# The first twenty projections of layer 0 in two halves of the contraction, with partial sums in DRAM and the second half's modulation on VectorE

## The chip, the cores and the metric

The kernel runs on one core of a Trainium2 chip. The metric is the time of one execution on the device in microseconds (us); the median of three runs is given. One execution was also recorded by the hardware profiler: its span runs from the first to the last instruction.

## What is computed

A trunk of two layers over 768 tokens (512 latent, 256 context) of width 2048. Cut to what matters here, each layer does this:

```python
shift, scale, gate = split(silu(c) @ ada_w + ada_b, 3)      # one vector for latent, one (c_ctx) for context tokens
h  = rms_norm(x, norm_w) * (1 + scale) + shift
p  = h @ w_in                                               # 2048 -> 8192 columns, split into twelve parts
y  = concat(gmlp(p), hgrn2_both_directions(p), diff_attention(p))
x  = x + gate * (y @ w_out)
```

The last layer's context output isn't needed, so many of its projections are 512 tokens wide, the rest and all of layer 0's are 768 wide. All of it is fp32: each matmul operand is split into a high and a low part, and a product is three matmuls (high x high, high weight x low, low weight x high).

## The kernel before

Activations lie transposed: a tile holds 128 features of all tokens. The contraction of 2048 is 16 tiles ("kt"), and the normalised, modulated input of a layer is 16 pairs hi0/lo0 to hi15/lo15. One projection makes 128 output columns for all tokens in an accumulator "pp" of 128x768 in PSUM (two of them): `mm_group` (line 383) issues, for each kt of a group of four, the three products, each as a matmul of 512 tokens and one of 256 with the same weights. That is 48 pairs for a projection. Weights come in quarters (four kt): a DMA into "raw", a ScalarE cast to "wh" (line 318), and a VectorE subtraction to "wl" (line 319), five buffers each.

Jobs of layer 0, in program order: four Hgrn units of five projections (two gates, query, output gate, value: projections 0 to 19), four Attn units of eight, the Gmlp unit, then 16 output projections. A unit's own work hangs on its projections. For Hgrn this is a scan in seven levels (lines 566 to 610): small TensorE products (line 581), masked copies and a product on VectorE (590, 599), three products on GpSimd (601, 603, 604) and a ScalarE copy back (569); then transposes and state products.

The modulation needs `silu(c) @ ada_w`, 24 blocks of 256 columns for each layer, 2 MB each. Layer 0's shift and scale (blocks 0 to 15) must be there before its h tiles. They run on TensorE (`ada_pe`, matmuls in line 250, then a VectorE copy in line 260 and lines 210 and 215 that finish the vector): two ahead of everything, then one for each kt while the first four projections run in the "lead", kt by kt, each four groups behind one new h tile (`h_tile`: VectorE 308, ScalarE 311, VectorE 312, for 512 and 256 tokens). The other 32 blocks (layer 0's gates and all of layer 1) run on VectorE (`ada_dve`, line 266): per block eight loads "adas" of 256 KB in two buffers, four accumulations (lines 275, 277) for each, a transpose (283) and a reduction (285). They are stepped as filler behind each job of layer 0, FILL steps of one kt each: 8 behind an Hgrn job, 7 Attn, 4 Gmlp, 9 behind an output projection.

A scheduler with a timing model sets the order of instructions on each engine; DMAs are issued by SyncE, in program order up to `pinned[0] = False`.

Of the kernel before, what the change touches and what calls it, by code (L numbers as in the profile page):

```python
# [33 lines left out]
MASKS = 5  # L34
FWD = (4, 5, 0, 1, 2, 3)
# [12 lines left out]
def trunk(  # L48
# [350 lines left out]

    yscr = [[dp.tile([P, T], F32, tag=f"y{l}_{j}", name=f"y{l}_{j}") for j in range(12)] for l in range(DEPTH)]  # L400
    xscr = [dp.tile([P, T], F32, tag=f"x1_{j}", name=f"x1_{j}") for j in range(KT)]
# [522 lines left out]
    UNPIN = 1  # L924
    SWAP = True
    TAILK = 2
    PREP = 16
    FILL = dict(Hgrn=8, Attn=7, Gmlp=4, Out=9)

    def advance(fill, n):  # L930
        for _ in range(n):
            if next(fill, 0) == 0:
                break

    def run_layer(l, xs, rb, pre, fillers, chain=None, ahead=()):
# [8 lines left out]
        acts = []  # L944
        lead = jobs[:LEAD]
# [5 lines left out]
        for g in range(4):  # L951
# [15 lines left out]
            for k in range(4):  # L967
# [3 lines left out]
                if kt < KT - TAILK:  # L971
                    for i in (0, 1, 2, 3) if l == 0 else (2, 3, 0, 1):
                        mm_group(pts[i], qs[i], acts, g, range(k, k + 1))
        for i in (0,2,1,3):
            mm_group(pts[i], qs[i], acts, 3, range(4 - TAILK, 4))
# [12 lines left out]
        rest = jobs[LEAD:]  # L988
        if SWAP:
            rest[0], rest[1] = rest[1], rest[0]  # L990
        nxt = fetch(rest[0])
        u0 = units[0]
        u0.gate(pts[0], 0)
        u0.silu_query(pts[2])
        u0.gate(pts[1], 1)
        u0.out_gate(pts[3])
        u0.levels()
        for i, j in enumerate(rest):
# [11 lines left out]
            if l == 0 and i == 0:  # L1010
                prepare_rest()
            if i == UNPIN:
                pinned[0] = False
            if i + 2 < len(rest):
                advance(fillers, FILL[type(owner[i + LEAD + (1 - 2 * i if SWAP and i < 2 else 0)]).__name__])
# [18 lines left out]
        for m in range(KT - TAILM):  # L1034
# [13 lines left out]
            advance(fillers, FILL["Out"] if m < KT - 3 else 1000 if m == KT - 3 else 0)  # L1048
# [56 lines left out]
    def pre0(i):  # L1105
        if i < KT:
# [101 lines left out]
```

## Time and profile before

| | |
|---|---|
| median of 3 runs | 2851.62 us (2851.58 to 2854.07) |
| span of the profiled execution | 2850.1 us |
| TensorE busy | 2786.3 us (98%) |
| VectorE busy | 1591.0 us (56%) |
| ScalarE busy | 967.0 us (34%) |
| GpSimd busy | 322.5 us (11%) |
| DMA | 316.29 MB, mean 111 GB/s |

The profile is of one execution, and its times run from the span's start. A matmul's record is longer than the distance to the next one, since matmuls are pipelined; what one costs is read from start to start. The Hgrn projections after the lead run from 163 to 491, attention to about 1208, the output projections of layer 0 from 1360 to 1636, layer 1 from there to the end.

### The profile page before, as it was taken

The page shows a single profiled execution, that of the slowest core. Times are in us where ns is not written, and L with a number is a line of the kernel's source. Part 1 is how long each engine was busy: PE and PEld are TensorE (multiplying, and loading weights), DVE is VectorE, ACT ScalarE, POOL GpSimd, SP SyncE. Part 2 cuts the span into 40 slices and gives each one's busy share as a digit, 9 for nine tenths or more (in the row PEclk, how much of TensorE's full clock was granted, in tenths as well). Part 3 has the DMA queues.
Part 4 walks back from the last instruction along what each step waited for, and adds up shares of the span by engine and source line. Part 5 has one row for each costly group of instructions (what it writes and reads, how often), then busy time and mean ns, then how long its engine had stood idle before and what let it go on. Part 6 is the DMA issues. An engine that isn't in the chain of part 4 may idle for free.

```text
span 2850.1 us, 47181 instructions
## 1 busy us (share of the span) xinstructions
PE 2786.3 (98%) x18724; PEld 2399.9 (84%) x18724; DVE 1591.0 (56%) x3256; ACT 967.0 (34%) x1855; POOL 322.5 (11%) x307
## 2 busy tenths in 40 slices
PE   6999999999999999999999999999999999999997
PEld 3678888888888888898888888888888888889786
DVE  4475677667667676624768664343343435344434
ACT  3233233234343343322311243333253535352421
POOL 0033023000000000001011013233000000001122
PEclk9999999999999999999999999999999999999998
DMA  9833433443333334333645422223222222224533
GB/s 354 273 108 85 121 103 112 120 123 90 113 94 104 104 94 122 100 92 118 204 149 161 118 70 64 63 65 75 67 74 60 73 67 66 74 79 136 154 98 93
DMA packets 168862, 316.29 MB, mean 111 GB/s; under 512 B 18240, under 2 KB 32704, under 8 KB 168640
## 3 DMA queue, kind: packets, MB, share of 16 engines
q1 hardware_dynamic: 168640, 313.27, 37.7%
q8 instruction: 147, 2.41, 0.3%
q14 instruction: 75, 0.61, 0.1%
HBM read 294.85 MB, written 18.35 MB: 110 GB/s over the span
## 4 chain that ended last, share of the span: by engine, by line
PE 92%; DVE 3%; issue 2%; DMA 2%; ACT 0%; SPq 0%; POOL 0%; DVEq 0%; POOLq 0%; ACTq 0%
PE pp L148 75%; PE pp L374 3%; PE a L808 3%; PE a L769 2%; PE a L497 2%; PE a L148 2%; PE a L250 1%; PE a L581 1%; PE a L374 1%; PE a L659 1%; DVE acc L277 1%; DMA adas<-in_ada_w_dram 1%; PE a L636 1%; SPq L69 0%; PE a L883 0%
## 5 line engine op out<-in xcount | busy, mean ns | idle before, releaser
L148 PE MATMUL pp<-hi,wh 128*128 128x512 f32 (+1 forms) x4016 | 1152.8, 350 | 4.0 <-ACT hi L311 3.4
L148 PE MATMUL pp<-lo,wh 128*128 128x512 f32 (+1 forms) x4016 | 1151.2, 348 | 0.6 <-DVE lo L312 0.6
L148 PE MATMUL pp<-hi,wl 128*128 128x512 f32 (+1 forms) x4016 | 1144.6, 348 | 0.0
L319 DVE TENSOR_TENSOR wl<-raw,wh 128x512 fp32r<-128x512 f32 x634 | 449.6, 711 | 673.6 <-ACT wh L318 641.4
L318 ACT CAST wh<-raw 128x512 fp32r<-128x512 f32 x634 | 392.1, 621 | 1200.1 <-PE pp L148 975.3
L148 PEld LDWEIGHTS pp<-hi,wh 128*128 128x128 f32 x4016 | 650.6, 189 | 111.5 <-ACT hi L311 6.8
L148 PEld LDWEIGHTS pp<-lo,wh 128*128 128x128 f32 x4016 | 651.5, 189 | 104.5 <-issue 5.0
L148 PEld LDWEIGHTS pp<-hi,wl 128*128 128x128 f32 x4016 | 647.9, 189 | 95.1
L277 DVE SCALAR_TENSOR_TENSOR acc<-adas,cc_s,acc 128x256 f32<-128x256 f32 x960 | 429.5, 496 | 68.3 <-DMA adas<-in_ada_w_dram 67.1
L817 POOL TENSOR_TENSOR ars<-e,mhalf 128x1 f32<-128x1 f32 x40 | 22.7, 568 | 1256.6 <-DVE e L815 1256.6
L780 ACT ACTIVATE C<-a,nb 128x256 f32<-128x256 f32 (+1 forms) x144 | 80.7, 567 | 67.5 <-DVE nb L776 65.4
L774 DVE TENSOR_REDUCE mx<-a 128x1 f32<-128x256 f32 (+1 forms) x144 | 72.6, 536 | 27.5 <-PE a L769 27.3
L808 PE MATMUL a<-A,WT 128*128 128x256 f32 x624 | 87.9, 282 | 0.0
L808 PEld LDWEIGHTS a<-A,WT 128*128 128x128 f32 x624 | 83.3, 190 | 3.6
L769 PE MATMUL a<-K,Q 128*128 128x256 f32 (+1 forms) x432 | 85.1, 335 | 0.0
L145 POOL TENSOR_TENSOR WT<-WT,T 128x768 f32<-128x768 f32 (+1 forms) x26 | 42.0, 1615 | 367.7 <-ACT T L144 367.7
L769 PEld LDWEIGHTS a<-K,Q 128*128 128x128 f32 x432 | 68.4, 188 | 9.2
L705 ACT COPY T<-pp 32x512 f32<-32x512 f32 x128 | 74.0, 578 | 1.9
L374 PE MATMUL pp<-wh,hi 128*128 128x256 f32 x256 | 73.5, 287 | 0.3 <-ACT K L478 0.2
L374 PE MATMUL pp<-wl,hi 128*128 128x256 f32 x256 | 73.2, 286 | 0.0
L374 PE MATMUL pp<-wh,lo 128*128 128x256 f32 x256 | 73.1, 286 | 0.0
L569 ACT COPY T<-A 128x768 f32<-128x768 f32 (+1 forms) x56 | 43.9, 784 | 85.0 <-POOL A L603 81.9
(226 smaller groups left out, 2315.9 us busy)
## 6 DMA issues: line engine op xcount, KB each, us to landing
raw<-in_w_in_dram SPq DMA_DIRECT2D x512, 256.0 KB, 2.9
adas<-in_ada_w_dram SPq DMA_DIRECT2D x256, 256.0 KB, 2.9
raw<-in_w_out_dram SPq DMA_DIRECT2D x128, 256.0 KB, 3.0
adaw<-in_ada_w_dram SPq DMA_DIRECT2D x42, 384.0 KB, 7.0
K<-in_ada_w_dram SPq DMA_DIRECT2D x28, 384.0 KB, 6.6
T<-y SPq DMA_DIRECT2D x12, 384.0 KB, 5.1
A<-in_xT_dram SPq DMA_DIRECT2D x8, 384.0 KB, 5.5
B<-in_xT_dram SPq DMA_DIRECT2D x8, 384.0 KB, 6.7
```

What stands on the lines that cost most here:

```text
L148: i = PE.matmul(*args, **kw)
L277: V.scalar_tensor_tensor(acc[:, i, :], wt[:, kt % 2, :], sca, acc[:, i, :], op0=ALU.mult, op1=ALU.add)
L318: S.copy(hi, src)
L319: V.tensor_tensor(lo, src, hi.bitcast(F32), op=ALU.subtract)
L374: PE.matmul(bank[:, c - a, :], x[:, cs], w[:, k, :], start=(kt == 0 and i == 0 and c % 2 == 0), stop=(kt == KT - 1 and i == 2), skip_group ...
L497: PE.transpose(pt[:, c - a, :], src[:, c * P : (c + 1) * P], ident)
L569: S.copy(km[:, :n].rearrange("p (j h i) -> p j h i", h=2, i=m), view(K2, 0, [[2 * m, n // (2 * m)], [T + m, 2], [1, m]]),)
L705: S.copy(sw[a : a + 32, :LAT], p[b : b + 32, :LAT])
L769: PE.matmul(pt[:, : hi - lo], a[:, qs], b[:, k0 + lo : k0 + hi], start=(i == 0), stop=(i == 2))
L774: V.tensor_reduce(mx[:, i : i + 1], pt[:, : hi - lo], axis=AX.X, op=ALU.max)
L780: S.activation(pr[:, m, lo:hi], pt[:, : hi - lo], AF.Exp, bias=nb, scale=SCALE, accum_out=sums[:, m, i : i + 1] if len(parts) == 2 else sm ...
L808: PE.matmul(po, a[:, c, :], b[:, c0 + c, :], start=(cnt == 0), stop=(cnt == 3 * nkc - 1))
```

## The change

In layer 0, the lead runs only kt 0 to 7, so only 8 modulation blocks are done by TensorE. The four partial sums are copied by ScalarE to SBUF and sent by its DMA queue to DRAM scratch. Sixteen more projections run their first half (kt 0 to 7) and are sent out likewise; behind each, 9 steps of a generator run on VectorE: the remaining 8 modulation blocks of shift and scale, and the h tiles 8 to 15 made from them. Then all twenty projections run their second half (kt 8 to 15); the partial sum is loaded back, VectorE adds it in PSUM, and the job's consumer follows as before, with 3 steps of filler. The mask table and the rope tables are prepared later. Layer 1's last eight modulation blocks move from layer 0's filler into layer 1's.

`mm_group` changes for every projection of both layers, in what is inner and outer: all products of a group for the 512 tokens, then all for the 256.

```diff
-    def mm_group(pt, wq, acts, g, ks=range(4), only=None):
+    def mm_group(pt, wq, acts, g, ks=range(4), only=None, first=0):
         wh, wl = wq
-        for k in ks:
-            kt = 4 * g + k
-            hi, lo = acts[kt]
-            for i, (w, a) in enumerate(((wh, hi), (wh, lo), (wl, hi))):
-                for dst, s in only or pt.ranges():
-                    shared = pt.host is not None and s.start == LAT
+        for dst, s in only or pt.ranges():
+            shared = pt.host is not None and s.start == LAT
+            for k in ks:
+                kt = 4 * g + k
+                hi, lo = acts[kt]
+                for i, (w, a) in enumerate(((wh, hi), (wh, lo), (wl, hi))):
                     pe_mm(
...
-                        start=(kt == 0 and i == 0 and not shared),
-                        stop=(kt == KT - 1 and i == 2),
+                        start=(kt == first and i == 0 and not shared),
+                        stop=(kt in (HALF - 1, KT - 1) and i == 2),
...
-    FILL = dict(Hgrn=8, Attn=7, Gmlp=4, Out=9)
+    FILL = {"Half": 3, 0: dict(Hgrn=8, Attn=7, Gmlp=4, Out=9), 1: dict(Hgrn=4, Attn=4, Gmlp=0, Out=0)}
+    LATE = 9
...
-        for g in range(4):
+        for g in range(2 if halves else 4):
...
+            def spill(i, pt):
+                t = g3("T3")
+                pt.act(t, AF.Copy, T)
+                S.dma_start(pscr[i], t)
+
+            def late_tiles():
+                for j in range(HALF, KT, 2):
+                    yield from ada_dve(l, j // 2)
+                    yield from ada_dve(l, (KT + j) // 2)
+                    for kt in (j, j + 1):
+                        acts.append(h_tile(l, kt, xs[kt], rb))
+                        yield
...
+            for i in range(LEAD, SPLIT):
+                pt = Proj(T)
+                for g in range(2):
+                    mm_group(pt, nxt[g], acts, g)
+                nxt = half(i + 1, 0) if i + 1 < SPLIT else half(0, 1)
+                spill(i, pt)
+                advance(late, LATE if i + 1 < SPLIT else 1000)
+            prepare()
+            part = part_load(0)
+            for i in range(SPLIT):
+                pt = Proj(T)
+                for g in range(2):
+                    mm_group(pt, nxt[g], acts, g + 2, first=HALF)
+                nxt = half(i + 1, 1) if i + 1 < SPLIT else fetch(jobs[SPLIT])
+                V.tensor_tensor(pt.ap[:, :T], pt.ap[:, :T], part, op=ALU.add)
+                if i + 1 < SPLIT:
+                    part = part_load(i + 1)
+                jobs[i][2](pt)
+                if i == 1:
+                    prepare_rest()
+                    pinned[0] = False
+                advance(fillers, FILL["Half"])
...
-        if i < KT:
+        if i < HALF:
             ada_pe(0, KT * (i % 2) + i - i % 2)
...
+    xs, rb, chain, ahead = run_layer(
+        0, xs, rb, pre0, itertools.chain(fill(0, range(16, 24)), fill(1, range(16)))
+    )
+    run_layer(1, xs, rb, lambda g: None, fill(1, range(16, 24)), chain, ahead)
```

How the order on the engines changes, at three places. On TensorE, the projection behind the lead, before (matmul, accumulator, activation tile and weights, with their buffer numbers):

```order
L148 MATMUL pp_308_1732<-hi0_77_366,wh_266_1419 128x512
L148 MATMUL pp_308_1732<-hi0_77_366,wh_266_1419 128x256
L148 MATMUL pp_308_1732<-lo0_78_367,wh_266_1419 128x512
L148 MATMUL pp_308_1732<-lo0_78_367,wh_266_1419 128x256
L148 MATMUL pp_308_1732<-hi0_77_366,wl_267_1420 128x512
L148 MATMUL pp_308_1732<-hi0_77_366,wl_267_1420 128x256
```

The same place now, from the last products of the 512 tokens of kt 2 on:

```order
L151 MATMUL pp_163_873<-hi2_99_521,wl_155_850 128x512
L151 MATMUL pp_163_873<-hi3_110_589,wh_154_849 128x512
L151 MATMUL pp_163_873<-lo3_111_590,wh_154_849 128x512
L151 MATMUL pp_163_873<-hi3_110_589,wl_155_850 128x512
L151 MATMUL pp_163_873<-hi0_77_386,wh_154_849 128x256
L151 MATMUL pp_163_873<-lo0_78_387,wh_154_849 128x256
L151 MATMUL pp_163_873<-hi0_77_386,wl_155_850 128x256
```

The two widths no longer alternate: twelve matmuls of 512 stand ahead of twelve of 256.

On VectorE, around h tiles 6 and 7 (T and lo), before ("a" is the result of a TensorE block in PSUM):

```order
L210 TENSOR_TENSOR adaT_94<-a_136_693,pack 128x4
L215 SCALAR_TENSOR_TENSOR gmul_96<-adaT_94,pack 128x4
L260 COPY T_154_790<-a_147_761 128x256
L308 SCALAR_TENSOR_TENSOR T_157_797<-B_11_166,gmul_96,WT_247 128x512
L308 SCALAR_TENSOR_TENSOR T_157_797<-B_11_166,gmul_96,WT_247 128x256
L312 SCALAR_TENSOR_TENSOR lo_156_796<-T_157_797,adaT_94,hi_155_795 128x512
```

And now:

```order
L218 SCALAR_TENSOR_TENSOR gmul_96<-adaT_94,pack 128x4
L280 SCALAR_TENSOR_TENSOR acc_937<-adas_944,cc_s,acc_937 128x256 x2
L311 SCALAR_TENSOR_TENSOR T_149_783<-B_11_186,gmul_96,WT_267 128x512
L311 SCALAR_TENSOR_TENSOR T_149_783<-B_11_186,gmul_96,WT_267 128x256
L311 SCALAR_TENSOR_TENSOR T_152_816<-B_11_186,gmul_96,WT_267 128x512
L311 SCALAR_TENSOR_TENSOR T_152_816<-B_11_186,gmul_96,WT_267 128x256
L280 SCALAR_TENSOR_TENSOR acc_937<-adas_944,cc_s,acc_937 128x256 x2
L315 SCALAR_TENSOR_TENSOR lo_148_782<-T_149_783,adaT_94,hi_147_781 128x512
```

The copy of the next TensorE block ahead of the tile is gone, and accumulations of the first VectorE block stand between.

On VectorE again, the levels of the first Hgrn unit in the second halves, now (1033 is the add of a partial sum, 322 the split of weights, 594 and 603 are the level's operations):

```order
L1033 TENSOR_TENSOR pp_2643<-pp_2643,K_432_2590 128x768
L322 TENSOR_TENSOR wl_3122<-raw_3119,wh_3121 128x512
L487 TENSOR_TENSOR T_453_2709<-pp_2643,T_452_2707 128x768
L549 TENSOR_TENSOR C_454_2711<-B_420_2513,T_453_2709 128x1536
L322 TENSOR_TENSOR wl_3128<-raw_3125,wh_3127 128x512
L566 TENSOR_TENSOR K_456_2715<-a_457_2716,fold 128x6x32
L594 COPY_PREDICATED K_456_2715<-mask,a_460_2745 128x6x32
L603 TENSOR_TENSOR C_454_2711<-C_454_2711,B_420_2513 128x2x384
L1033 TENSOR_TENSOR pp_2994<-pp_2994,K_451_2705 128x768
L322 TENSOR_TENSOR wl_3292<-raw_3289,wh_3291 128x512
L594 COPY_PREDICATED K_456_2715<-mask,a_462_2777 128x6x32
L603 TENSOR_TENSOR C_454_2711<-C_454_2711,K_458_2742 128x2x192x2
```

Adds of later projections stand between the levels of a unit.

## Rows read from the trace of the kernel before

**Rows 1.** The page: busy time of the engines (with their share of the span and number of instructions), and the shares of the chain that ended last by engine.

```profile
PE 2786.3 (98%) x18724; PEld 2399.9 (84%) x18724; DVE 1591.0 (56%) x3256; ACT 967.0 (34%) x1855; POOL 322.5 (11%) x307
...
PE 92%; DVE 3%; issue 2%; DMA 2%; ACT 0%; SPq 0%; POOL 0%; DVEq 0%; POOLq 0%; ACTq 0%
```

**Rows 2.** The windows: start and end, length, busy time of each engine (instructions), granted TensorE clock, DMA share, GB/s.

```profile
0.00:46.00 46.00, 18.23 (x141) 8.19 (x144) 25.25 (x42) 19.35 (x26) 2.66 (x10) 0.90 0.98 363
46.00:163.00 117.00, 112.75 (x835) 77.29 (x829) 51.01 (x111) 28.15 (x51) 0.00 (x0) 1.00 0.75 252
163.00:188.00 25.00, 21.40 (x241) 18.36 (x242) 21.95 (x33) 8.30 (x13) 12.13 (x9) 0.86 0.45 142
188.00:491.30 303.30, 301.78 (x2995) 262.02 (x2994) 208.34 (x426) 99.43 (x193) 84.20 (x82) 1.00 0.37 104
491.30:1208.00 716.70, 716.70 (x4412) 631.12 (x4411) 500.52 (x1174) 260.70 (x546) 13.77 (x22) 1.00 0.37 107
1700.00:2850.00 1150.00, 1129.72 (x7116) 973.99 (x7114) 481.06 (x885) 418.88 (x816) 169.97 (x160) 0.99 0.31 82
```

**Rows 3.** The timeline of VectorE around h tiles 6 and 7 (start, length, engine, line, operation, tiles, count, idle time before and who ended it), and the matmuls of one modulation block on TensorE.

```profile
84.59 0.16 DVE L215 SCALAR_TENSOR_TENSOR gmul<-adaT,pack 128x4 f32<-128x4 f32 x1
91.49 0.42 DVE L260 COPY T<-a 128x256 f32<-128x256 f32 x1 [6.74 <-PE a L250]
91.83 1.14 DVE L308 SCALAR_TENSOR_TENSOR T<-B,gmul,WT 128x512 f32<-128x512 f32 x2
...
96.09 1.14 DVE L312 SCALAR_TENSOR_TENSOR lo<-T,adaT,hi 128x256 fp32r<-128x256 f32 x2
...
121.45 1.46 PE L250 MATMUL a<-K,sc 128*32 128x256 f32 x18
```

**Rows 4.** Groups of instructions by line (count, busy time, mean ns of one, idle time before), and of the DMA issues the loads of modulation weights for VectorE (count, KB each, us to landing).

```profile
L277 DVE SCALAR_TENSOR_TENSOR acc<-adas,cc_s,acc 128x256 f32<-128x256 f32 x960 | 429.5, 496 | 68.3 <-DMA adas<-in_ada_w_dram 67.1
L319 DVE TENSOR_TENSOR wl<-raw,wh 128x512 fp32r<-128x512 f32 x634 | 449.6, 711 | 673.6 <-ACT wh L318 641.4
...
L283 DVE STREAM_TRANSPOSE T<-acc 128x512 f32<-128x512 f32 x32 | 22.5, 704 | 0.6 <-DVE acc L277 0.5
L285 DVE TENSOR_REDUCE red<-T 128x16 f32<-128x512 f32 x32 | 21.7, 677 | 0.2
L476 ACT COPY T<-pp 128x768 f32<-128x768 f32 x24 | 19.2, 800 | 0.1
L483 DVE TENSOR_TENSOR T<-pp,T 128x768 f32<-128x768 f32 (+2 forms) x15 | 11.9, 794 | 3.1 <-ACT T L478 3.0
...
adas<-in_ada_w_dram SPq DMA_DIRECT2D x256, 256.0 KB, 2.9
```

**Rows 5.** The dense stretch of VectorE's filler from 400 to 450: the window for all engines, the window of line 277 alone (VectorE's busy time and count, clock, DMA share, GB/s), and instructions of VectorE and GpSimd in it.

```profile
400.00:450.00 50.00, 50.00 (x321) 44.16 (x320) 45.01 (x111) 11.02 (x26) 3.17 (x2) 1.00 0.50 148
...
400.00:450.00 50.00, 30.78 (x68) 1.00 0.50 148
...
423.06 1.67 DVE L277 SCALAR_TENSOR_TENSOR acc<-adas,cc_s,acc 128x256 f32<-128x256 f32 x4 [1.06 <-DMA adas<-in_ada_w_dram]
424.65 0.68 DVE L319 TENSOR_TENSOR wl<-raw,wh 128x512 fp32r<-128x512 f32 x1
...
436.92 2.14 DVE L277 SCALAR_TENSOR_TENSOR acc<-adas,cc_s,acc 128x256 f32<-128x256 f32 x1
...
436.94 1.83 POOL L547 TENSOR_TENSOR T<-A 128x768 f32<-128x768 f32 x1 [7.34 <-ACT A L478]
```

**Rows 6.** TensorE's matmuls in four regular runs, the first and the last row of each: one width of 512 (layer 1; 28 steps lie between the two), one width of 256 (the end of layer 1; 51 steps), and alternating pairs, where a row holds a pair, with ten pairs between the first two and fourteen between the other two.

```profile
2719.62 0.39 PE L148 MATMUL pp<-hi,wl 128*128 128x512 f32 x1
...
2725.97 0.39 PE L148 MATMUL pp<-hi,wh 128*128 128x512 f32 x1
...
2805.80 0.28 PE L148 MATMUL pp<-hi,wl 128*128 128x256 f32 x1
...
2811.92 0.28 PE L148 MATMUL pp<-hi,wl 128*128 128x256 f32 x1
...
902.11 0.52 PE L148 MATMUL pp<-hi,wh 128*128 128x512 f32 x2
...
905.58 0.51 PE L148 MATMUL pp<-lo,wh 128*128 128x512 f32 x2
...
2408.22 0.52 PE L148 MATMUL pp<-lo,wh 128*128 128x512 f32 x2
...
2413.16 0.52 PE L148 MATMUL pp<-hi,wh 128*128 128x512 f32 x2
```

**Rows 7.** The levels of the third Hgrn unit: two of its level products on TensorE, and GpSimd's operations between them.

```profile
376.20 0.63 PE L581 MATMUL a<-C,T 128*32 128x32 f32 x48
...
378.17 0.64 POOL L604 TENSOR_TENSOR K<-B 128x48 f32<-128x48 f32 x1 [3.04 <-DVE C L599]
...
379.70 0.84 POOL L603 TENSOR_TENSOR A<-A,K 128x384 f32<-128x384 f32 x1
...
381.78 0.63 PE L581 MATMUL a<-C,T 128*32 128x32 f32 x48
```

**Rows 8.** TensorE's timeline behind its stop in the first Hgrn unit.

```profile
180.91 0.87 PE L581 MATMUL a<-C,T 128*32 128x32 f32 x48 [3.60 <-DVE C L599]
...
183.37 0.84 PE L148 MATMUL pp<-hi,wh 128*128 128x512 f32 x2
```

More of the change, by code (lines that the diff above doesn't have):

```diff
@@ L1 @@
+import itertools
 import math
@@ L34 @@
 MASKS = 5
+HALF = KT // 2
+SPLIT = 20
 FWD = (4, 5, 0, 1, 2, 3)
@@ L400, in trunk @@
     yscr = [[dp.tile([P, T], F32, tag=f"y{l}_{j}", name=f"y{l}_{j}") for j in range(12)] for l in range(DEPTH)]
+    pscr = [dp.tile([P, T], F32, tag=f"p0_{j}", name=f"p0_{j}") for j in range(SPLIT)]
     xscr = [dp.tile([P, T], F32, tag=f"x1_{j}", name=f"x1_{j}") for j in range(KT)]
@@ L933, in advance, with part_load @@
                 break
+    def part_load(i):
+        t = g3("K3")
+        load(t, pscr[i])
+        return t
     def run_layer(l, xs, rb, pre, fillers, chain=None, ahead=()):
@@ L944, in run_layer @@
         acts = []
+        halves = l == 0
         lead = jobs[:LEAD]
@@ L970, in run_layer @@
                 acts.append(h_tile(l, kt, xs[kt], rb))
-                if kt < KT - TAILK:
+                if halves or kt < KT - TAILK:
                     for i in (0, 1, 2, 3) if l == 0 else (2, 3, 0, 1):
                         mm_group(pts[i], qs[i], acts, g, range(k, k + 1))
-        for i in (0,2,1,3):
-            mm_group(pts[i], qs[i], acts, 3, range(4 - TAILK, 4))
+        if not halves:
+            for i in (0,2,1,3):
+                mm_group(pts[i], qs[i], acts, 3, range(4 - TAILK, 4))
         n = L.n
@@ L986, in out_act, with half @@
             return hi, lo
[L988 to L997, printed above, removed]
+        if halves:
+            def half(i, h):
+                return [w_quarter(w_in[l, jobs[i][0]], g) for g in (2 * h, 2 * h + 1)]
+            def spill(i, pt):
[9 more added lines that the diff above has]
+                        yield
+            late = late_tiles()
+            nxt = half(LEAD, 0)
+            for i in range(LEAD):
+                spill(i, pts[i])
+            for i in range(LEAD, SPLIT):
[20 more added lines that the diff above has]
+                advance(fillers, FILL["Half"])
+            rest = jobs[SPLIT:]
+            pos = SPLIT
+        else:
+            rest = jobs[LEAD:]
+            pos = LEAD
+            if SWAP:
+                rest[0], rest[1] = rest[1], rest[0]
+            nxt = fetch(rest[0])
+            u0 = units[0]
+            u0.gate(pts[0], 0)
+            u0.silu_query(pts[2])
+            u0.gate(pts[1], 1)
+            u0.out_gate(pts[3])
+            u0.levels()
@@ L1116, in trunk, with fill @@
         pre0(i)
-    def fill():
-        for l, b0 in ((0, 16), (1, 0)):
-            for b in range(b0, 24):
-                yield from ada_dve(l, b)
-    xs, rb, chain, ahead = run_layer(0, xs, rb, pre0, fill())
-    run_layer(1, xs, rb, lambda g: None, iter(()), chain, ahead)
+    def fill(l, blocks):
+        for b in blocks:
+            yield from ada_dve(l, b)
+    xs, rb, chain, ahead = run_layer(
+        0, xs, rb, pre0, itertools.chain(fill(0, range(16, 24)), fill(1, range(16)))
+    )
+    run_layer(1, xs, rb, lambda g: None, fill(1, range(16, 24)), chain, ahead)
 def _rope_tables():
```

12 lines of the change are left out of this document (2 added, 10 removed).

## Prediction

> **What bounds the kernel now.** I read the page first. TensorE is busy 2786.3 of 2850.1 us and holds 92% of the chain that ended last [rows 1]. The windows say where the other two per cent lie: 27.8 us before 46, while the first modulation weights stream at a DMA share of 0.98; 4.3 us to 163; 3.6 us to 188, where the granted clock is also down to 0.86; then next to nothing for 300 us and nothing at all for the 717 us behind them [rows 2]. So there are three things to win: TensorE work that another engine could do, the waits of the first 190 us, and a better rate of matmuls that look busy already. VectorE has room: 208 of 303 us in the Hgrn stage, 481 of 1150 in the second layer [rows 2].
>
> The start in detail [rows 3]: h tile 6 stands on VectorE behind the copy of the ninth TensorE block, at 91.49 after 6.74 us of waiting, though the scale it needs was there at 84.59. One TensorE block is 32 matmuls at (1.46 − 0.41)/17 = 0.062 us, so 2.0 us of TensorE and 2 MB of weights.
>
> **The change part by part.** The sum runs along the time of the last lo15, then the end of projection 19 (the last Hgrn one, at 491.3 before: the window's border), then the rest.
>
> *Lead, kt 0 to 7.* Blocks 9 to 16 leave TensorE: 8 × 2.0 = 16 us. Without the ninth block, h6 and h7 follow 84.59 at once; a tile is 1.14 us, ScalarE's step and 1.14 us again, so lo7 comes at about 90 instead of 97.2 (96.09 + 1.14) [rows 3], and the last four lead groups (4 × 3 × 0.347 = 4.2 us [rows 6]) end near 95.
>
> *Eight blocks on VectorE.* From about 83 until lo15, the order has on VectorE 64 modulation tiles of four L277-like operations, 37 weight splits, 10 h tiles, 8 transposes with their reductions. A tile costs 424.65 − 423.06 = 1.59 us from start to start [rows 5], so 64 × 1.6 = 102; splits 37 × 0.68 = 25 [rows 4]; h tiles 10 × 2.3 = 23; 8 × (0.70 + 0.68) = 11 [rows 4]. That is 161 us of work, so lo15 not before 83 + 161 + 9 = 253. But only two buffers hold such tiles, and a transfer takes 2.9 us to land [rows 4]; where little else stands between, VectorE waits for it, as by 1.06 us in the dense stretch [rows 5]. Played through by hand over the new order, with 3.1 us from the last use of a buffer to its next, two blocks with what stands between take 43.5 us instead of 39.4. Four such pairs, some 2 us of late start and about 12 us of last h tiles and splits: 83 + 174 + 12 = 269; I take **268**. The other bound is the pace of the dense stretch, 50 us for 17 tiles (68 operations) or 2.94 each [rows 5]: 83 + 64 × 2.94 + 12 = 283. My value lies between, nearer to the hand count, because the dense stretch carried Hgrn work that the first halves don't have.
>
> *Sixteen first halves* on TensorE meanwhile. 24 matmuls of 512 at 0.2267 and 24 of 256 at 0.120 us are 8.32 us [rows 6]; 16 × 8.32 = 133, from 95 to 228. So VectorE is the bound of this stretch, and TensorE waits some 40 us there in small pieces. The ScalarE copies into scratch (20 × 0.80 [rows 4]) and their DMAs on ScalarE's queue stand ahead of weight casts there; that queue's issue price isn't in the trace, SyncE's is nothing to a few tenths. ScalarE was a third busy in the Hgrn window [rows 2], so I cost it at nothing; at 1 us each the 16 would still fit into 40 us of slack. 20 × 0.39 MB written and read again are 16 MB over 400 us, 40 GB/s beside 104 at a share of 0.37 [rows 2]: hidden.
>
> *Second halves.* At 268 the order has TensorE some 6 us from the end of projections 0 and 1; then 18 × 8.32 = 150. The stages' own matmuls up to projection 19 are the same number of rows as before: 328.3 us (163 to 491.3) less 16 × 16.64 (48 pairs of 0.3467 [rows 6]) less 5.1 us idle [rows 2] less 3.5 lost at the halved clock (25 us at 0.86 are 7 us at half speed) less about 6 of irregular pairs (below) leave 48; I take 50. So 474 without any wait. Waits: each half now ends in an add of 128x768 with PSUM on VectorE, nearest row 0.79 us [rows 4], 16 us in all, ahead of the consumers; behind it stand weight splits and level operations. TensorE has two accumulators and 8.3 us until it needs this one back, so an add in time is free. In the first unit VectorE has about 60 us of work beside 54 of TensorE, later some 45. I take 18 us of waits in all, from nothing to 40. Projection 19 then ends at 492, where it ended at 491.3: the removed TensorE blocks and the early start pay for the VectorE-bound stretch, no more.
>
> *Order within a group*, in every projection of both layers. Pairs of 512 and 256 ran in two ways: ten in 3.47 us (0.347 each, the sum of the pure rates) or fourteen in 4.94 (0.353) [rows 6]. Runs of one width keep 0.2267 and 0.120. Behind 491 there are 82 projections that alternate, so at most 82 × 48 × 0.0066 = 26 us, at least 0. Summing the starts of these pairs over the trace I find about three quarters in the slow way: **−20 us**.
>
> *Fill.* Eight modulation blocks move into layer 1, four steps behind each of the first projections. That is 8 × 13 = 104 us more for a VectorE that is 42% busy there [rows 2], and splits and softmax steps stand behind them. 0 to 8 us; I take 2.
>
> Sum: 2850.1 + 0.7 − 20 + 2 = 2833; the median stands 1.5 us over the profiled span (2851.62 against 2850.1), so **2834 us**.
>
> **The rivals.**
>
> 1. *Slower: the Hgrn levels come to light.* Seven levels lie between the unit's first small products and its transposes; before, some 30 us of projections and 5 of other TensorE work hid them, in the new order 14.5 and 5. Each level goes TensorE L581, VectorE, GpSimd, ScalarE, TensorE. L581 starts at 376.20, GpSimd resumes at 378.17 behind VectorE's line 599, ends at 380.54, and a ScalarE copy and an L581 (381.78) follow [rows 7]. If every level needs such a turn of 5.6 us, seven take 39 against 19.5, 19 us more for each of four units, 76 in all, and with 10 of the 18 us counted already 2834 + 66 = **2900**. For it: GpSimd's wait of 3.04 us on VectorE. Against: TensorE had no idle time before these L581, so its order placed them, and by the code what GpSimd makes at 379.70 feeds a level two further on, so a turn can serve two or three levels, 2.8 us each or less, just within the 19.5. The kernel gets slower than before from some 3.8 us a level.
>
> 2. *VectorE's stretch runs at 2.94 us a tile.* lo15 at 283, **2850**. For it: the waits of rows 5.
>
> 3. *Grouping brings nothing*, since the slow pairs have another cause (a weight load, a bank) that stays: the change then doesn't do what this part does here. **2854**.
>
> 4. *No waits* in the second halves, lo15 at 256: 2834 − 18 − 12 = **2804**.
>
> 5. *The clock.* TensorE stood still for 3.60 us ahead of 180.91, the pairs of matmuls behind it took 0.84 us instead of 0.51 [rows 6, 8], and the granted clock of that window is 0.86, some 7 us at the lower level; over the lead's 4.3 us of smaller gaps it is 1.00 [rows 2]. If the 40 us of waiting fall into one gap of about 3 us for each half, each half takes 8.32 + 3.5 = 11.8 us, 16 of them 189: TensorE becomes the bound and lo15's matmuls come at about 284, **2848 to 2860** with some of it in the second halves. By the Trainium skill, "TensorE: Matmul & The Clock Gate", section "HAM oscillation — how this bites in real kernels", a loop that waits between short bursts of matmuls falls to the lower clock again and again and pays for each return; the one gap of 3.60 us here agrees, the lead doesn't show it.
>
> A rule that bears on rival 1: by the Trainium skill, "SBUF — State Buffer", section "Who interferes with whom", a VectorE operation with two SBUF inputs contends with a GpSimd operation that reads SBUF. The trace agrees: one accumulation beside a GpSimd operation took 2.14 us instead of the mean of 0.50 [rows 4, 5]; the sums stand without it.
>
> **How the numbers follow.** Forecast 0.47, rival 1 0.15, rival 2 0.12, rival 4 0.12, rival 5 0.08, rival 3 0.06. 0.2% (5.7 us) is about what a measurement of this kernel can tell from no change: 2845.9 to 2857.3 counts as the same. The forecast's own spread, 2818 to 2852, puts 0.40 in faster and 0.07 in same; rival 4 is faster; rival 1 gives 0.13 to slower and 0.02 to same; rivals 2, 3 and 5 give 0.06 to faster, 0.11 to same, 0.09 to slower. Faster 0.58, same 0.20, slower 0.22. The range leaves out most of rival 1 above and half of rival 4 below: 2810 to 2868.
>
> **What would show it.** In the changed profile: the last lo15 between 256 and 283; TensorE with gaps, and VectorE without, between 95 and 268; the end of projection 19 within 480 to 510; line 581 every 2.8 us or so with TensorE waits in front of it under 5 us a unit; matmuls of one width 227 and 120 ns apart throughout, so that from projection 19 to the end the program is 15 to 25 us shorter; the granted clock at 1.00 over the first halves, or else rival 5. The forecast is wrong if waits in front of L581 or for VectorE's add exceed 40 us, or if the stages behind 492 don't shrink.

## The result and the profile after

The changed kernel took 2893.67 us (median of 4 runs, 2892.80 to 2894.38) beside 2852.85 for the kernel before (4 runs): a ratio of 1.0146, 95% interval 1.0133 to 1.0160. It is 41 us **slower**; forecast were 2834 and at most 2868. The profiled execution spans 2892.1 us. Lines of the code moved down by three or four: L148 of before is L151 now, L277 is L280, L319 is L322, L581 is L585, L599 is L603.

First where the time went, by three points of the program that both traces have:

| end of (us from the span's start) | before | after | difference | forecast after |
|---|---|---|---|---|
| projection 19 (the next one's first matmul) | 491.1 | 532.6 | +41.5 | 492 |
| layer 0's attention and Gmlp (first Out projection) | 1360.4 | 1400.6 | +40.2 | |
| layer 1's lead | 1699.2 | 1739.5 | +40.3 | |
| the span | 2850.1 | 2892.1 | +42.0 | 2833 |

The whole loss is there when projection 19 ends; behind it the two kernels take the same time to within two microseconds, where 18 us were to be won. The page of the changed kernel (busy time, instructions, and the chain of waits), which answers to [rows 1]:

```profile
PE 2770.4 (96%) x18500; PEld 2407.1 (83%) x18500; DVE 1705.9 (59%) x3538; ACT 980.2 (34%) x1875; POOL 326.6 (11%) x307
PE 87%; DVE 4%; DMA 4%; issue 2%; POOL 1%; ACT 1%; SPq 0%; DVEq 0%; POOLq 0%; ACTq 0%
```

TensorE is 16 us less busy, and the program is longer: there are more waits, and TensorE's part of the chain fell from 92 to 87%. The 16 are a net figure: eight blocks of some 2.0 us are gone, the order within a group saves some, and matmuls at a lower clock take longer (below). The windows by stage (stretch, its length, busy time of PE, PEld, DVE, ACT and POOL with instructions, granted clock, DMA share, GB/s), beside [rows 2]; 94 is the end of the half lead, 274 that of the last first half, 298.6 that of the second halves of projections 0 and 1, 532.5 that of projection 19:

```profile
94.00:274.00 180.00, 150.09 (x824) 127.68 (x824) 137.30 (x316) 38.71 (x62) 0.00 (x0) 0.91 0.53 169
274.00:298.60 24.60, 20.66 (x108) 17.24 (x108) 21.58 (x56) 11.59 (x20) 0.00 (x0) 0.86 0.78 270
298.60:532.50 233.90, 206.66 (x2535) 181.19 (x2533) 171.42 (x298) 87.84 (x171) 96.55 (x90) 0.93 0.35 107
532.50:1248.00 715.50, 714.64 (x4404) 634.29 (x4405) 487.85 (x1141) 258.93 (x543) 14.91 (x24) 1.00 0.35 104
```

TensorE stood still for 29.9, 3.9 and 27.2 us in the first three, 61 in all, and in these stretches its clock was below 1.00. Before, the same part of the program had under 10 us of idle time. So there are two places to explain: 94 to 298.6, and 298.6 to 532.5.

**The first place.** The waits of 95 to 285 (who waited, line, for whom; us in total, times, longest):

```profile
ACT wh L321 <- DMA raw<-in_w_in_dram: 76.4, 17, 9.4
PE pp L151 <- ACT wh L321: 26.8, 6, 7.1
DVE acc L280 <- DMA adas<-in_ada_w_dram: 21.4, 23, 2.3
DVE wl L322 <- ACT wh L321: 12.6, 13, 3.2
DVE adaT L213 <- PE a L291: 8.0, 3, 3.6
```

VectorE, the bound of this stretch by forecast, waits 21.4 us for modulation tiles, and another 20.6 us for ScalarE's casts and for the small matmuls that finish a block (the last two lines). TensorE waits for casts, and the casts for **weights from DRAM**. Why the weights are late stands in SyncE's timeline (start, duration, operation) and, below it, in its own waits of the same stretch:

```profile
132.48 16.75 SPq L72 DMA_DIRECT2D adas<-in_ada_w_dram  x5
149.32 1.03 SPq L72 DMA_DIRECT2D raw<-in_w_in_dram  x2
...
SPq L72 <- DVE acc L280: 121.7, 57, 8.6
```

Five modulation loads take 16.75 us to issue, because each has to wait until VectorE gives one of the two buffers back; the next two weight loads stand behind them on the same queue. ScalarE and TensorE pay:

```profile
154.10 1.26 ACT L321 CAST wh<-raw 128x512 fp32r<-128x512 f32 x2 [5.58 <-DMA raw<-in_w_in_dram]
```

```profile
147.40 0.28 PE L151 MATMUL pp<-hi,wl 128*128 128x256 f32 x1
154.77 0.80 PE L151 MATMUL pp<-hi,wh 128*128 128x512 f32 x1 [7.09 <-ACT wh L321]
```

And the granted clock falls in that stop (windows around it, columns as above):

```profile
140.00:147.60 7.60, 7.60 (x46) 6.62 (x44) 7.06 (x17) 2.34 (x5) 0.00 (x0) 1.00 0.43 147
147.60:154.80 7.20, 0.11 (x2) 0.04 (x1) 4.59 (x13) 1.48 (x3) 0.00 (x0) 0.67 0.66 200
154.80:160.30 5.50, 5.50 (x14) 4.34 (x15) 5.43 (x12) 0.55 (x1) 0.00 (x0) 0.50 0.31 98
160.30:170.00 9.70, 9.70 (x66) 8.56 (x66) 7.66 (x20) 2.05 (x3) 0.00 (x0) 1.00 0.66 198
```

0.50 is the lower level, 1.2 GHz: it set in within the 7.1 us of standing still (0.67 over that window), and TensorE then worked for 5.5 us at half speed. The last lo tiles come at 287 (VectorE's line 315, four in a row), where 268 was forecast:

```profile
287.38 2.20 DVE L315 SCALAR_TENSOR_TENSOR lo<-T,adaT,hi 128x512 fp32r<-128x512 f32 x4
```

**The second place.** TensorE's waits of 300 to 540:

```profile
PE a L585 <- DVE C L603: 11.1, 9, 2.0
PE a L585 <- ACT T L573: 8.4, 3, 2.8
PE pp L151 <- ACT T L480: 7.8, 4, 2.8
```

L585 is the Hgrn levels' small matmuls. One unit on TensorE's timeline; the level matmuls 48 at a time, with nothing between them, until a projection can start again:

```profile
394.03 0.62 PE L585 MATMUL a<-C,T 128*32 128x32 f32 x48 [0.38 <-DVE C L603]
397.46 0.87 PE L585 MATMUL a<-C,T 128*32 128x32 f32 x48 [2.81 <-ACT T L573]
400.33 0.87 PE L585 MATMUL a<-C,T 128*32 128x32 f32 x48 [2.00 <-DVE C L603]
402.17 0.80 PE L151 MATMUL pp<-hi,wh 128*128 128x512 f32 x1 [0.98 <-ACT T L480]
```

ScalarE in the same microseconds (L573 copies for a level, L482 is the output gate's sigmoid, L480 the copy of the value projection):

```profile
396.53 0.83 ACT L573 COPY T<-A 128x768 f32<-128x768 f32 x1 [2.34 <-POOL A L607]
...
399.89 0.83 ACT L573 COPY T<-A 128x768 f32<-128x768 f32 x1
400.63 0.80 ACT L482 ACTIVATE T<-pp 128x768 f32<-128x768 f32 x1
401.33 0.79 ACT L480 COPY T<-pp 128x768 f32<-128x768 f32 x1
```

VectorE had added the stored half to the output gate's accumulator at 383.82, in 0.97 us:

```profile
383.82 0.97 DVE L1033 TENSOR_TENSOR pp<-pp,K 128x768 f32<-128x768 f32 x1
392.93 0.95 DVE L603 TENSOR_TENSOR C<-C,B 128x768 f32<-128x768 f32 x1
```

So that accumulator was ready by 384.8 and is read at 400.63 (and once more by the product behind it), and the value's copy comes behind the sigmoid. For 16 us one of the two accumulators is held by a sigmoid whose target is one of four T3 buffers, which the level copies use too and ahead of it. TensorE has finished the other, stands in front of the levels, and goes on when the value's copy is done, at 402.12. The clock falls here as well: 0.58 over 394.6 to 402.2 and 0.66 over the 5.8 us behind.

### The profile page after: what moved, and what is told of

Its sections match the earlier page's. It is cut to its first block, busy times and chain, and to the rows that moved or that the text cites. A ratio compares the mean times of both kernels' runs of the same rounds, so it can differ in the third digit from the quotient of the medians.

```text
span 2892.1 us, 47193 instructions
## 1 busy us (share of the span) xinstructions
PE 2770.4 (96%) x18500; PEld 2407.1 (83%) x18500; DVE 1705.9 (59%) x3538; ACT 980.2 (34%) x1875; POOL 326.6 (11%) x307
## 4 chain that ended last, share of the span: by engine, by line
PE 87%; DVE 4%; DMA 4%; issue 2%; POOL 1%; ACT 1%; SPq 0%; DVEq 0%; POOLq 0%; ACTq 0%
PE pp L151 71%; PE pp L377 3%; PE a L812 3%; PE a L773 2%; PE a L501 2%; DMA adas<-in_ada_w_dram 2%; DVE acc L280 2%; PE a L151 1%; DMA raw<-in_w_in_dram 1%; PE a L377 1%; PE a L663 1%; PE a L253 1%; PE a L585 1%; PE a L640 1%; DMA T<-y 1%
## 5 line engine op out<-in xcount | busy, mean ns | idle before, releaser
L151 PE MATMUL pp<-hi,wh 128*128 128x512 f32 (+1 forms) x4032 | 1408.5, 350 | 43.5 <-ACT wh L321 26.8
L151 PE MATMUL pp<-lo,wh 128*128 128x512 f32 (+1 forms) x4032 | 1408.7, 350 | 1.4 <-DVE lo L315 1.4
L151 PE MATMUL pp<-hi,wl 128*128 128x512 f32 (+1 forms) x4032 | 1404.5, 349 | 0.8 <-DVE wl L322 0.8
L151 PEld LDWEIGHTS pp<-hi,wh 128*128 128x128 f32 x4032 | 768.5, 191 | 145.8 <-ACT wh L321 28.0
L151 PEld LDWEIGHTS pp<-lo,wh 128*128 128x128 f32 x4032 | 769.7, 191 | 98.3 <-issue 2.8
L151 PEld LDWEIGHTS pp<-hi,wl 128*128 128x128 f32 x4032 | 768.1, 191 | 96.4 <-DVE wl L322 3.0
L322 DVE TENSOR_TENSOR wl<-raw,wh 128x512 fp32r<-128x512 f32 x634 | 452.9, 716 | 605.8 <-ACT wh L321 589.0
L280 DVE SCALAR_TENSOR_TENSOR acc<-adas,cc_s,acc 128x256 f32<-128x256 f32 x1200 | 521.8, 485 | 85.0 <-DMA adas<-in_ada_w_dram 84.2
L148 POOL TENSOR_TENSOR WT<-WT,T 128x768 f32<-128x768 f32 (+1 forms) x26 | 41.6, 1600 | 365.1 <-ACT T L147 365.1
L573 ACT COPY T<-A 128x768 f32<-128x768 f32 (+1 forms) x56 | 43.7, 781 | 78.7 <-POOL A L607 76.9
```

What stands on the lines that cost most here:

```text
L151: i = PE.matmul(*args, **kw)
L280: V.scalar_tensor_tensor(acc[:, i, :], wt[:, kt % 2, :], sca, acc[:, i, :], op0=ALU.mult, op1=ALU.add)
L322: V.tensor_tensor(lo, src, hi.bitcast(F32), op=ALU.subtract)
L573: S.copy(km[:, :n].rearrange("p (j h i) -> p j h i", h=2, i=m), view(K2, 0, [[2 * m, n // (2 * m)], [T + m, 2], [1, m]]),)
```

## Experiments

Runs that share a chip share the kernel before, whose median was 2851.33, 2851.10 or 2852.41 there. Ratios are to it. The intervals of experiments 2, 4, 7 and 9 overlap that of the changed kernel, so a difference of 6 us or less from it is shown weakly at best.

**1. before_grouped**: the kernel before, with the order of matmuls in a group alone.

```
-        for k in ks:
-            ...
-            for i, (w, a) in enumerate(((wh, hi), (wh, lo), (wl, hi))):
-                for dst, s in only or pt.ranges():
+        for dst, s in only or pt.ranges():
+            for k in ks:
+                ...
+                for i, (w, a) in enumerate(((wh, hi), (wh, lo), (wl, hi))):
```

> The kernel before, with nothing changed but the order inside a group (all products for 512 tokens, then all for 256). The forecast's step (three quarters of the pairs run at 0.353 instead of 0.347 us because the widths alternate): 20 us less, about 2832 us. The rival, to which the changed kernel's trace points (the first matmuls of 512 behind any interruption take 0.23 to 0.24 us whatever the order is): 0 to 5 us less, 2847 to 2853 us.

Measured 2840.74 (5 runs), ratio 0.9961 (0.9948 to 0.9974): 10.6 us faster, half of the term. It is the fastest kernel of this study.

**2. after_alternating**: the changed kernel with the old order of matmuls, the same diff the other way round.

```
+        for k in ks:
+            ...
+                for dst, s in only or pt.ranges():
```

> The changed kernel with the two widths alternating again in every group, all else as changed. If grouping is worth 20 us and something else has eaten it: about 2913 us. If grouping is worth next to nothing: 2893 to 2898 us.

2899.72, ratio 1.0169 (1.0154 to 1.0184): 6 us longer than the changed kernel. Experiments 1 and 2 agree on the sign and put the term at 6 to 11 us. About half of the −20 was never there.

**3. after_short_late_blocks**: the late modulation blocks on VectorE take two of their sixteen steps, so 56 of the 64 tiles, their loads and most of that sum are left out.

```
-                    yield from ada_dve(l, j // 2)
-                    yield from ada_dve(l, (KT + j) // 2)
+                    yield from ada_dve(l, j // 2, 2)
+                    yield from ada_dve(l, (KT + j) // 2, 2)
```

> The changed kernel with the eight late modulation blocks cut to 2 of their 16 contraction tiles, so most of that sum is left out (56 of 64 weight tiles, some 90 us of VectorE). Theory: VectorE's stretch bounds the first halves and the time of lo15; without it the sixteen halves end near 96 + 133 = 230 instead of 274, the second halves start 45 to 55 us earlier, 2838 to 2848 us. Rival: the first halves wait for something else (ScalarE's casts, the scratch writes), and the loss lies in the second halves alone: above 2875 us.

2863.07, ratio 1.0040 (1.0026 to 1.0054): 31 us shorter than the changed kernel. The second halves start at 249.85, 24 us earlier, where 45 to 55 were expected. The first stretch is now denser (10.2 of 156 us idle), while the second halves look as in the changed kernel (windows from 94 and from 250):

```profile
94.00:250.00 156.00, 145.77 (x848) 125.73 (x848) 70.76 (x150) 44.36 (x75) 0.00 (x0) 0.96 0.43 144
250.00:502.00 252.00, 224.47 (x2629) 196.96 (x2627) 176.74 (x313) 94.11 (x177) 93.37 (x90) 0.93 0.34 104
```

So the two places are two causes: taking VectorE's work and its loads out of the first cures most of the first alone.

**4. after_permuted_halves**: the second halves in another order, so that gates and queries of two units stand between the levels.

```
+SEQ = (0, 1, 2, 5, 6, 3, 4, 7, 10, 11, 8, 9, 12, 15, 16, 13, 14, 17, 18, 19)
...
-            for i in range(SPLIT):
+            for at, i in enumerate(SEQ):
```

> The changed kernel with the second halves in another order: the next unit's two gate projections stand between a unit's query and its output gate and value, so four halves (33 us) lie between the start of the seven levels and the products that need them, instead of two (17 us). Theory: TensorE's waits in front of line 585 (some 6 us in each unit) and the halved clock behind them go: 25 to 40 us less, 2853 to 2868 us. Rival: these waits come from VectorE's adds and splits ahead of the level operations, or the levels' place on TensorE moves with the order: 2885 to 2895 us.

2899.92, ratio 1.0166 (1.0151 to 1.0181), 6 us longer. The theory that the order of the projections alone hides the levels is not borne out: TensorE still waits 16.5 us ahead of the level matmuls, and the accumulator's 7.1 us are there too.

**5. after_gate_without_temp**: the output gate's sigmoid goes straight into its final buffer; no T3 buffer.

```
-            sg = g3("T3")
-            p.act(sg, AF.Sigmoid, n)
             self.y = g3("WT")
-            p.mul(self.y, sg, n, hn_s[L.l][:, 0:1])
+            p.act(self.y, AF.Sigmoid, n)
+            p.mul(self.y, self.y, n, hn_s[L.l][:, 0:1])
```

> The changed kernel with one thing different: the Hgrn output gate's sigmoid is written into its result tile (WT) and multiplied there, so it no longer needs one of the four T3 buffers that the level copies turn over. In the changed kernel the sigmoid stands on ScalarE behind all seven level copies, so the accumulator of the output gate is held for 17 us after its matmuls and TensorE, with both accumulators held, has nothing but levels to run. Theory: that hold, not the levels themselves, makes TensorE wait; the waits in the second halves (31 us with those behind line 585, and some 13 us of halved clock) mostly go: 25 to 45 us less, 2850 to 2868 us. Rival, the forecast's own slow case (a level takes over 2.8 us whatever else runs): TensorE waits in front of line 585 all the same, 2885 to 2895 us.

2884.75, ratio 1.0117 (1.0102 to 1.0132): 9 us shorter, where 25 to 45 were expected. The sigmoid now runs ahead of the level copies (ScalarE's timeline), and the waits ahead of L585 fell from 19.5 to 1.7 us (TensorE's waits of 295 to 545):

```profile
379.62 0.82 ACT L482 ACTIVATE WT<-pp 128x768 f32<-128x768 f32 x1 [0.15 <-PE a L501]
380.32 0.83 ACT L573 COPY T<-A 128x768 f32<-128x768 f32 x1
```

```profile
PE a L640 <- DVE K L629: 9.0, 2, 6.3
...
PE a L585 <- DVE C L603: 1.7, 1, 1.7
```

So the levels as such were not the limit here. But half of what those waits had cost went to a new wait, 9.0 us, of L640 for VectorE's L629. What VectorE did ahead of that (its timeline):

```profile
412.47 0.88 DVE L280 SCALAR_TENSOR_TENSOR acc<-adas,cc_s,acc 128x256 f32<-128x256 f32 x2 [1.17 <-DMA adas<-in_ada_w_dram]
417.99 1.67 DVE L280 SCALAR_TENSOR_TENSOR acc<-adas,cc_s,acc 128x256 f32<-128x256 f32 x4 [0.49 <-DMA adas<-in_ada_w_dram]
420.18 0.68 DVE L629 COPY K<-a 128x512 f32<-128x512 f32 x1
```

It is the modulation of later stages, three steps behind each half, which wait for DMAs while the unit's own copy stands behind them.

**6. after_split_24**: 24 projections in halves instead of 20, one step of late modulation less behind each first half.

```
-SPLIT = 20
+SPLIT = 24
...
-    LATE = 9
+    LATE = 8
```

> The changed kernel with 24 instead of 20 projections in halves (two attention gates and two keys more), and 8 instead of 9 steps behind each first half. Theory: VectorE bounds the first halves, TensorE waits there 30 us and more in gaps of up to 7 us; four more halves (33 us) fill these and come off the rest: 20 to 33 us less, 2860 to 2873 us. Rival: VectorE's additional splits, copies and adds lengthen its stretch by as much: 2885 to 2895 us.

2879.64, ratio 1.0103 (1.0088 to 1.0118): 14 us shorter. TensorE has more to do while VectorE sets the pace (158.8 of the 180 us from 94 to 274, beside 150.1).

**7. after_loads_unpinned**: the pinning of loads is lifted ahead of the first halves instead of in the second ones.

```
             late = late_tiles()
+            pinned[0] = False
...
                     prepare_rest()
-                    pinned[0] = False
```

> The changed kernel with SyncE's loads free of program order from the end of the lead on instead of from the second of the second halves. In the changed kernel a weight load for the next half stands on SyncE behind a modulation load that waits for VectorE to give a buffer back. Theory: that order makes TensorE's gaps of 2 to 7 us in the first halves (and so the halved clock there), but the end of the stretch is VectorE's, so the gain is small: 0 to 12 us less, 2881 to 2893 us. Rival: the gaps hold up VectorE as well (it waits 13 us for casts and 8 for TensorE there): 15 to 25 us less, 2868 to 2878 us.

2888.00, ratio 1.0129 (1.0112 to 1.0146): 6 us shorter by the medians. TensorE's waits for casts are gone, but its wait for the last modulation blocks' sums (L291 for VectorE's L288) is 27.1 us in four, one of 16.65 us. Late weights alone thus cost little: when they are early, TensorE runs ahead and then waits for VectorE.

**8. after_three_buffers**: three buffers for modulation tiles instead of two, four for raw weights instead of five.

```
-                wt = wp.tile([P, 2, 256], F32, tag="adas", bufs=2, name=nm("adas"))
+                wt = wp.tile([P, 2, 256], F32, tag="adas", bufs=3, name=nm("adas"))
...
-        raw = wp.tile([P, 4, P], F32, tag="raw", bufs=5, name=nm("raw"))
+        raw = wp.tile([P, 4, P], F32, tag="raw", bufs=4, name=nm("raw"))
```

> The changed kernel with three instead of two buffers for the modulation tiles of VectorE; to make room, four instead of five buffers for raw weights. In the first halves VectorE was idle 45 of 200 us, 24 of them waiting for a modulation tile. Theory: the third buffer takes most of these waits away, lo15 comes 15 to 25 us earlier: 2868 to 2880 us. Rival: the transfers, or the raw buffer that is missing, hold it up instead: 2888 us or more.

2880.82, ratio 1.0102 (1.0087 to 1.0117): 13 us shorter, though one weight buffer is gone. VectorE's waits of the same stretch:

```profile
DVE wl L322 <- ACT wh L321: 19.6, 16, 3.5
DVE acc L280 <- DMA adas<-in_ada_w_dram: 6.7, 6, 2.7
```

The waits for tiles fell from 21.4 to 6.7 us, half of that came back as waits for casts, and the second halves start at 258 instead of 274.

**9. after_warm_matmuls**: 16 and 8 matmuls without use ahead of the last two levels, to keep the clock up.

```
+                if L.l == 0 and lv > 4:
+                    for _ in range(16 if lv == 5 else 8):
+                        PE.matmul(
...
```

> The changed kernel with useless matmuls added in each Hgrn unit of layer 0, 16 of 192 columns and 8 of 384 (some 2.9 us a unit), into the PSUM tiles of the last two levels ahead of their own products, where TensorE stops for 2.8 and 2.0 us. In the changed kernel 7 to 10 us at half clock follow each of these stops, 34 us in the four units. Theory: that halved clock costs 8 to 14 us in all, and matmuls in the gap keep it up: although 12 us of work are added, 2880 to 2890 us. Rival: the stops count only for their own length, the added work is free at best: 2893 to 2905 us.

2897.52, ratio 1.0153 (1.0138 to 1.0168): 4 us longer by the medians. Inconclusive: they came to stand one stop too late, the stop of 2.8 us stayed, and the clock fell behind it as before. The clock's share is not settled by it.

**10. after_gate_no_half_filler**: experiment 5, and no modulation of later stages beside the second halves; it is done beside attention instead (nine steps for seven).

```
-    FILL = {"Half": 3, 0: dict(Hgrn=8, Attn=7, Gmlp=4, Out=9), 1: ...}
+    FILL = {"Half": 0, 0: dict(Hgrn=8, Attn=9, Gmlp=4, Out=9), 1: ...}
```

> The kernel with the gate's sigmoid written in place (2884.75 us), and besides no filler steps behind the second halves (0 instead of 3), 9 instead of 7 behind attention's projections. There, VectorE still had modulation tiles in the Hgrn units, with waits for their transfers, ahead of partial-sum adds, level products and copies that TensorE waited for (a 6.34 us stop behind a copy). Theory: VectorE's filler is what is left of the second halves' loss: 8 to 18 us less, 2867 to 2877 us. Rival: the adds, splits and level operations alone fill VectorE's queue, or the filler is missed later: 2880 us or more.

2867.96, ratio 1.0051 (1.0034 to 1.0068): 17 us less than experiment 5, 26 less than the changed kernel. From 300 to 532 TensorE now idles 9.3 of 232 us at a granted clock of 0.98 (after, in the same stretch: 26.7 at 0.93). This kernel's window, of an execution that took 2874.6 us, the longest of its four:

```profile
300.00:532.00 232.00, 222.69 (x2571) 194.71 (x2569) 123.16 (x197) 89.04 (x171) 94.71 (x90) 0.98 0.28 84
```

**11. after_all_mended**: experiments 6, 8 and 10 together.

> All that helped in one: 24 projections in halves, the gate's sigmoid in place, no filler behind second halves, three buffers for modulation tiles with four for raw weights. If the gains are of separate causes they add up: 2893.7 less 14, 9, 13 and some 10 makes 2848 us, about the kernel before; if they overlap (a later second stage gains from the same waits), 2855 to 2870 us. To beat the grouped kernel before (2840.74 us) it would have to gain 7 us more than the sum.

2850.53 (10 runs), ratio 0.9997 (0.9988 to 1.0007): 43 us shorter than the changed kernel, as long as the kernel before. The parts were −14, −13 and −26, 53 in all, so they overlap a little. What is left of the first place, and of the second:

```profile
94.00:274.00 180.00, 167.76 (x954) 142.88 (x953) 142.50 (x329) 45.88 (x74) 0.00 (x0) 0.96 0.58 190
300.00:550.00 250.00, 235.67 (x2711) 207.00 (x2710) 130.81 (x201) 99.91 (x191) 97.06 (x91) 0.97 0.28 82
```

**12. before_fill_in_layer_1**: the kernel before, with the modulation blocks 16 to 23 of layer 1 computed in layer 1, as in the changed one.

```
-    xs, rb, chain, ahead = run_layer(0, xs, rb, pre0, fill())
-    run_layer(1, xs, rb, lambda g: None, iter(()), chain, ahead)
+    xs, rb, chain, ahead = run_layer(0, xs, rb, pre0, fill((0, 16, 24), (1, 0, 16)))
+    run_layer(1, xs, rb, lambda g: None, fill((1, 16, 24)), chain, ahead)
```

> The kernel before, with only the filler moved as in the change: layer 1's last eight modulation blocks computed behind layer 1's own projections, four steps each. The forecast's step: 0 to 8 us more, 2 taken, 2853 us; in the changed kernel's trace layer 1 lasted 1152.4 instead of 1150.7 us while its groups were regular, which in the grouped kernel before gave it 1149.8: 2.6 us more, 2853 to 2855 us. Rival: fewer blocks in layer 0 give back as much there: 2851 us.

2856.97 (10 runs) beside 2852.41, ratio 1.0017 (1.0007 to 1.0026): 4.6 us longer.

## Why the prediction was wrong

Its terms, step by step. The forecast was 60 us short: 24.6 at the end of projections 0 and 1 (298.6 for 274), 16 in the eighteen second halves (234 for 218), 19 behind them.

**The lead** was right: 94 for "near 95", with eight of TensorE's blocks out of it.

**lo15 at 268**: wrong, it came between 287 and 290, beyond rival 2's 283. The work was counted right: VectorE is busy 159.8 us from 83 to 290, where 161 were forecast from 83 on:

```profile
83.00:290.00 207.00, 172.90 (x939) 146.11 (x938) 159.78 (x371) 50.64 (x83) 0.00 (x0) 0.90 0.56 181
```

What was mis-sized is its idle time, 47 us in that window, where 268 − 83 − 161 leaves 24. I had played VectorE's own buffers through, 4.1 us for each of four pairs of blocks, and those waits came out near that, 21.4 us for 16. I took for granted that casts and small matmuls would always be there when VectorE asked for them; they cost 20.6 us more. The step that failed is the sentence that TensorE "waits some 40 us there in small pieces", put at no cost. Its size was near: up to the end of projections 0 and 1 TensorE stood still for 33.8 us, where 180 us less 18 halves leave 30. But the pieces were not small (up to 7.1 us), the clock fell in them, and the engines that wait for TensorE waited too. The copies into scratch, also put at nothing, held TensorE once in this stretch, for 2.5 us. TensorE, ScalarE and VectorE wait for one another in a ring here: VectorE frees a modulation buffer, SyncE may then issue the next load and the weight load behind it, ScalarE casts it, VectorE splits it, TensorE multiplies. The prediction priced each engine and took a queue's issues as "nothing to a few tenths"; the queue's **order** was part of the price. Experiment 8 shows the ring from one side (a buffer more: −13), experiment 3 from the other (less VectorE work: −31), and experiment 7 that the weights' place alone is worth 6 at most.

**The stops and the clock** (rival 5, given 0.08). It happened, beside the waits of VectorE: behind stops of 2.8 and 7.1 us the clock was at its lower level, and 0.86 to 0.93 were granted over the three windows, which makes some 72 us at that level. TensorE was busy 377.4 us from 94 to 532.5; 36 halves of 8.32 are 300, and with the estimate of 50 for the stages' own matmuls 350. The forecast's 398 us from 94 to 492 so held 350 of work and 48 of standing still; it came to 377 and 61. Counted on TensorE, then, 27 of the 40 us that were lost here are matmuls that took longer, and only 13 are more standing still. Nearly all of the 27 can be the clock: by my estimate from windows of half a microsecond TensorE worked some 48 us at the lower level, which cost 24, about 15 of them ahead of 298.6 and 8 behind. The forecast's sum had nothing for it. The clock is no cause apart from the stops, since it fell in them. By the Trainium skill, "TensorE: Matmul & The Clock Gate", section "HAM oscillation — how this bites in real kernels", bursts with waits between them pay for each return to full speed: the trace agrees, 5.5 us at half speed behind the stop at 147.6. How much of the first place's part would be won with the same stops at full speed is open, since VectorE bounds that place and experiment 9 did not place its matmuls well.

**The second halves**, 18 us of waits: TensorE idled 27 us in 298.6 to 532.5, and the time came out 16 us over: 9 of more standing still and about 8 of clock. The term's size was near, but its cause was not in the sum. "TensorE has two accumulators and 8.3 us until it needs this one back, so an add in time is free": the add was in time (0.97 us, done by 384.8), the *reader* behind it was not, at 400.63. I had followed the accumulator only to the add. A projection of 16.64 us had covered such a late reader before: there the sigmoid, L478, stood behind the level copies too, and TensorE was busy for all of the 42 us around it (ScalarE's timeline and the window):

```profile
380.57 0.83 ACT L569 COPY T<-A 128x768 f32<-128x768 f32 x1 [3.64 <-POOL A L603]
...
381.83 0.80 ACT L478 ACTIVATE T<-pp 128x768 f32<-128x768 f32 x1
...
360.00:402.00 42.00, 42.00 (x525) 35.90 (x512) 28.65 (x53) 15.66 (x29) 16.49 (x19) 1.00 0.32 87
```

One of 8.32 doesn't cover it. Rival 1 had the right place, L585 in sight and stops of 2 to 2.8 us, but not the mechanism: experiment 5 left the seven levels as they are, changed the output gate's buffer, and the waits ahead of L585 fell to 1.7 us. Experiment 10 shows the second cover that was gone, VectorE's modulation of later stages; both together are worth 26 us. The prediction had set that work aside with "about 60 us of work beside 54", which gives a busy time and no place in the queue.

A rule weighed beside rival 1 held: VectorE's L603, with two inputs in SBUF, took 0.95 us alone (392.93) and 2.23 beside GpSimd operations that read SBUF:

```profile
381.51 1.47 POOL L608 TENSOR_TENSOR K<-B 128x768 f32<-128x768 f32 x1
381.56 2.23 DVE L603 TENSOR_TENSOR C<-C,B 128x768 f32<-128x768 f32 x1
```

By the Trainium skill, "SBUF — State Buffer", section "Who interferes with whom", a VectorE operation with two SBUF inputs contends with a GpSimd operation that reads SBUF; these rows agree. That it did not set the time is argued, not shown: in experiment 5 the waits for L603 are down to 1.7 us, but its longest L603 took only 1.48.

**Grouping, −20**: mis-sized. The whole program gains 10.6 (experiment 1) or 6 (experiment 2), and not all of it where the −20 were placed: in experiment 1's profiled execution the first attention product starts 4.1 us earlier (634.46 for 638.57) and the end comes 8.4 us earlier, so about half of the gain lies behind projection 19. The step that failed is that runs of one width keep 0.2267 us each. TensorE's timeline in the changed kernel's second layer:

```profile
1436.82 0.40 PE L151 MATMUL pp<-hi,wh 128*128 128x512 f32 x1
1437.05 0.40 PE L151 MATMUL pp<-lo,wh 128*128 128x512 f32 x1
1437.29 0.39 PE L151 MATMUL pp<-hi,wl 128*128 128x512 f32 x1
```

The starts are 0.23 and 0.24 us apart, though every matmul here has 512 columns. The slow pairs that I counted were not slow by the change of width alone; rival 3's "another cause that stays" holds for about half of them. Which cause is open.

**Fill, +2**: measured +4.6, within its bounds of 0 to 8. It and the grouping's share behind projection 19, some 4 us, nearly cancel, so the last 2360 us look unchanged.

**What the change won** is real and stays in experiment 11: eight blocks off TensorE and an earlier start. With the waits found here made shorter (12 and 14 us of standing still are left in its two windows), that and the order of matmuls just pay for what halving costs; the order alone, without halves, is 10 us better.

## What to carry to other kernels

When a step is cut in half, everything that hid behind it must fit in half the time: follow each accumulator and each buffer to its **last reader**, not to the first operation on it, and see what stands ahead of that reader on its engine. A sum of busy times per engine bounds a stretch from below only; where engines share a few buffers and one in-order queue of loads, the first load that waits for a buffer holds back the loads of all others. Ask also how long the single stops are, and not only what they add up to: in this kernel 13 us more of standing still than forecast came with an estimated 24 us lost to the lower clock. And a change of several parts is to be run part by part: the loop order, a few lines, was worth 10.6 us by itself, and the rest cost 48 (experiment 2 beside the kernel before).

## What was not expected of the hardware

Matmuls of one width, in a row, start 0.23 to 0.24 us apart in some places and 0.227 in others; a run of small matmuls or a change of width stands ahead of the slower ones that I looked at. An issue on SyncE's queue, costed at a few tenths of a microsecond, took 16.75 us for five when their buffer was in use.
